# The scheduler orders the instructions of a two-layer diffusion trunk by its detailed timeline model in place of its simple one

## The chip, the cores and the metric

The kernel runs on one core of one Trainium2 chip. The metric is device time in microseconds. One execution was taken by the hardware profiler; the others were only timed.

## The reference

Two layers of a trunk are computed for two token groups that share one set of parameters: 128 context tokens and 512 latent tokens (a grid of 64 columns and 8 rows), 1024 features each. Cut to what matters, one layer is:

```
mod = silu(c) @ ada_w + ada_b                 # six vectors of 1024: shift, scale, gate, twice
h   = rms_norm(x) * (1 + scale) + shift
z   = h @ w_in                                # 2560 columns
ya  = bidirectional RG-LRU(conv(z), gate)     # sigmoid gates, exp, sqrt, two scans
yb  = neighbourhood attention (4 heads of 64) # the context tokens: plain attention
yc  = differential attention (4 heads, two components of 32)
x  += gate * (concat(ya, yb, yc) @ w_out)
u   = conv3(h2 @ ffn_up)                      # 5632 columns
x  += gate * ((gelu(u_gate) * u_val) @ ffn_down)
```

The outputs are the tokens of both groups, the final LRU states and the keys and values of the context tokens.

## The kernel before

Tokens lie along the free dimension: the residual stream `xt` holds the 1024 features as 8 tiles of 128 partitions by 640 tokens. Products are made with fp32r operands that are split into a high and a low part. For a weight, `unit` (L372) does this: ScalarE copies the raw weight into `wh`, VectorE subtracts it to get `wl`, each 128x1024, and each product then takes three matmuls (L272 to L274, L281 to L283, L1286 to L1288).

The mixer (`mixer`, L597) runs the LRU for four column groups (`lru_conv`, `lru_gates`, `lru_decay`, `lru_scan`, L666 to L725), the projections by 256 columns (`tok_chunk`, L817), the two attentions (`na_prompt` L959, `na_sample` L974, `df_run` L1135) and the output product. Its weights come as a list of 14 jobs, `jobs`, each a load and one or two units; `prep` starts the next one while the one before is in use. The FFN (`ffn`, L1227) first treats three column tiles directly and then, in a loop of 19 iterations per layer, computes one tile of 2x128 columns of `ffn_up` in seven partial products (`Up`, L1270, p1 to p7), a convolution and gelu (`conv`, L1330), and a part of `ffn_down` for the tiles made earlier (`d_quad`, L1373). The next tile's weights are prepared by `up_weights` (L569), the last of them in `Up.rest` (L1276). The product that makes the modulation (`ada_group`, L210) is spread over the mixer and the FFN as matmuls with four narrow weights side by side.

All loads go through SyncE's queue. Raw weights of all kinds (`raw_tile`, L93) share one tag with two buffers, intermediate tiles of 640 tokens share a tag with eight, and PSUM is split into 3 + 2 + 2 + 1 banks (m, s, t, and one for ada and o).

The order of the instructions isn't the program's text. The framework records the instructions, and when its context closes, it plays them through a model of the chip: whenever an engine is free there, it gets the ready instruction that has the smallest priority number, and a tile gets its buffer at that moment. The order in which each engine got its instructions becomes the program of that engine. The priority number counts up along the text. The kernel moves it with `later`:

```
def later(n):
    tc.cur_priority += n
    yield
    tc.cur_priority -= n
```

The offsets reach from -2000 for the products of a head after the first (`run`, L200) over -40 for `Up.rest` and +40 for `conv` to +700 for the second pair of `lru_scan`. `tc.issue_after(x)` keeps what a block issues on the engine of x behind x, and `act` (L657) chains the LRU's activations in one order. All of these are constraints or weights in the scheduler's choice; where they leave a choice open, the model's times decide which instruction is ready when an engine comes free.

## Time and profile before

| what | value |
|---|---|
| median of 3 runs | 1601.61 us (1600.32 to 1602.11) |
| the profiled execution's own time | 1599.11 us |
| its span, first to last instruction | 1597.3 us |
| instructions | 28596 |
| mean granted clock of TensorE | 0.995 |

The profiled execution is 2.5 us shorter than the median of the runs, and 1.8 us of its time lie outside the span. The engines are TensorE (PE, its weight loads PEld), VectorE (DVE), ScalarE (ACT), GpSimd (POOL) and SyncE (SP; SPq is its queue). A busy time adds up the stretches in which at least one instruction of the engine runs. Matmuls are pipelined, so one is shown longer than the distance to the next.

### The profile page before, as it was taken

How to read it: one execution, taken by the hardware profiler on the slowest of the kernel's cores; microseconds unless marked ns; L12 is line 12 of the kernel's file. 1: busy time of each engine (PE TensorE's matmuls, PEld its weight loads, DVE VectorE, ACT ScalarE, POOL GpSimd, SP SyncE). 2: the span in 40 equal slices, each digit the busy share in tenths (PEclk: the TensorE clock that was granted, in tenths of full speed). 3: DMA queues.
4: the chain of work that ended last, by engine and by line, in shares of the span. 5: the costliest groups of instructions: out<-in, count | busy, mean ns of one | idle time of the engine just before them, and what ended most of it. 6: DMA issues, size and time to landing. Idle time of an engine off the chain costs nothing.

```text
span 1597.3 us, 28596 instructions
## 1 busy us (share of the span) xinstructions
PE 1552.9 (97%) x11183; PEld 1453.3 (91%) x11183; DVE 1321.2 (83%) x2894; ACT 917.2 (57%) x1689; POOL 89.9 (6%) x78
## 2 busy tenths in 40 slices
PE   7999999899999999999999899999999999999998
PEld 6877788799999999999998777988999999999998
DVE  5886778978999888888897776788799998888884
ACT  5865558746655454445458666685466554444451
POOL 0310200100000000000012201010000000000000
PEclk8999999999999999999999999999999999999999
DMA  9556632121444333222244564220312322222221
GB/s 329 182 196 219 174 108 87 47 80 37 142 153 137 99 89 89 80 77 73 90 145 132 185 215 126 70 106 29 89 54 73 116 80 80 80 80 80 73 73 67
DMA packets 208069, 177.30 MB, mean 111 GB/s; under 512 B 47574, under 2 KB 197310, under 8 KB 201790
## 3 DMA queue, kind: packets, MB, share of 16 engines
q1 hardware_dynamic: 207934, 175.48, 35.6%
q8 instruction: 88, 1.44, 0.4%
q14 instruction: 47, 0.39, 0.1%
HBM read 165.12 MB, written 10.34 MB: 110 GB/s over the span
## 4 chain that ended last, share of the span: by engine, by line
PE 78%; DVE 9%; ACT 5%; DMA 4%; issue 3%; POOL 1%; SPq 1%; DVEq 0%; ACTq 0%; POOLq 0%
PE m L283 6%; PE m L281 6%; PE m L282 6%; PE m L1286 6%; PE m L1287 6%; PE m L1288 5%; PE s L283 4%; PE s L282 4%; PE s L281 4%; PE m L272 3%; PE m L274 3%; PE m L273 3%; PE t L1288 3%; PE t L1286 3%; PE t L1287 3%
## 5 line engine op out<-in xcount | busy, mean ns | idle before, releaser
L117 DVE TENSOR_TENSOR wl<-up,wh 128x1024 fp32r<-128x1024 f32 x126 | 153.6, 1223 | 40.5 <-ACT wh L110 39.6
L110 ACT ACTIVATE wh<-up 128x1024 fp32r<-128x1024 f32 x126 | 132.2, 1052 | 81.6 <-PE t L1288 40.3
L1344 DVE SCALAR_TENSOR_TENSOR u<-raw,vec,u 128x127 f32<-128x127 f32 x352 | 175.4, 544 | 0.8 <-ACT u L1338 0.8
L272 PE MATMUL m<-wh,h 128*128 128x256 f32 x480 | 140.0, 292 | 0.0
L274 PE MATMUL m<-wh,h 128*128 128x256 f32 x480 | 138.2, 288 | 0.0
L273 PE MATMUL m<-wl,h 128*128 128x256 f32 x480 | 137.2, 286 | 0.0
L281 PE MATMUL m<-act,wh 128*128 128x320 f32 (+2 forms) x376 | 116.8, 311 | 0.0
L282 PE MATMUL m<-act,wl 128*128 128x320 f32 (+2 forms) x376 | 116.5, 310 | 0.0
L283 PE MATMUL m<-act,wh 128*128 128x320 f32 (+2 forms) x376 | 116.4, 310 | 0.0
L281 PE MATMUL s<-act,wh 128*128 128x320 f32 (+2 forms) x376 | 116.3, 309 | 0.0
L283 PE MATMUL s<-act,wh 128*128 128x320 f32 (+2 forms) x376 | 116.2, 309 | 0.0
L282 PE MATMUL s<-act,wl 128*128 128x320 f32 (+2 forms) x376 | 115.9, 309 | 0.0
L283 PE MATMUL m<-h,wh 128*128 128x320 f32 (+2 forms) x352 | 111.7, 319 | 2.9 <-DVE h L117 1.7
L281 PE MATMUL m<-h,wh 128*128 128x320 f32 (+2 forms) x352 | 111.3, 317 | 1.0 <-DVE xt L541 0.7
L282 PE MATMUL m<-h,wl 128*128 128x320 f32 (+2 forms) x352 | 110.9, 315 | 0.0
L541 DVE SCALAR_TENSOR_TENSOR xt<-m,mod,xt 128x128 f32<-128x128 f32 (+3 forms) x224 | 90.5, 432 | 16.7 <-PE m L283 15.8
L272 PEld LDWEIGHTS m<-wh,h 128*128 128x128 f32 x480 | 91.7, 191 | 12.9 <-issue 11.6
L274 PEld LDWEIGHTS m<-wh,h 128*128 128x128 f32 x480 | 91.6, 191 | 3.2 <-issue 2.7
L1286 PE MATMUL m<-h,wh 128*128 128x320 f32 x304 | 94.4, 311 | 0.0
L273 PEld LDWEIGHTS m<-wl,h 128*128 128x128 f32 x480 | 91.7, 191 | 2.9 <-issue 2.9
L1288 PE MATMUL t<-tx,wh 128*128 128x320 f32 x304 | 94.1, 310 | 0.0
L1286 PE MATMUL t<-tx,wh 128*128 128x320 f32 x304 | 94.1, 310 | 0.0
(371 smaller groups left out, 4948.9 us busy)
## 6 DMA issues: line engine op xcount, KB each, us to landing
up<-in_ffn_up_dram SPq DMA_DIRECT2D x88, 512.0 KB
adaw<-in_ada_w_dram SPq DMA_DIRECT2D x40, 1024.0 KB
w<-in_w_in_dram SPq DMA_DIRECT2D x16, 1024.0 KB
rawd<-in_ffn_down_dram SPq DMA_DIRECT2D x24, 512.0 KB
pro<-in_ada_w_dram SPq DMA_DIRECT2D x30, 256.0 KB
w<-in_w_out_dram SPq DMA_DIRECT2D x8, 768.0 KB
rawd<-in_ffn_down_dram SPq DMA_DIRECT2D x16, 384.0 KB
xd<-xt SPq DMA_DIRECT2D x4, 1280.0 KB
```

The source lines that it names most:

```text
L110: return nc.scalar.activation(out, in_, AF.Copy)
L117: (eng or nc.vector).tensor_tensor(out, a, b, op=OP.subtract)
L272: nc.tensor.matmul(out, st[0], mv[0], start=(i == 0), stop=False)
L273: nc.tensor.matmul(out, st[0], mv[1], start=False, stop=False)
L274: nc.tensor.matmul(out, st[1], mv[0], start=False, stop=(i == n - 1))
L281: nc.tensor.matmul(out, a[0], b[0], start=(k == total[0]), stop=False)
L282: nc.tensor.matmul(out, a[1], b[0], start=False, stop=False)
L283: last = nc.tensor.matmul(out, a[0], b[1], start=False, stop=(k == total[-1]))
L1286: nc.tensor.matmul(ps, st[0], mv[0], start=first and k == 0, stop=False, skip_group_check=chk)
L1287: nc.tensor.matmul(ps, st[1], mv[0], start=False, stop=False, skip_group_check=chk)
L1288: nc.tensor.matmul(ps, st[0], mv[1], start=False, stop=last and k == 3, skip_group_check=chk)
L1344: nc.vector.scalar_tensor_tensor(u[:, oa:ob], r[:, oa + sft:ob + sft], w, u[:, oa:ob], op0=OP.mult, op1=OP.add)
```

## The change

The context in which the framework schedules gets one argument. With it, the framework plays the instructions through its detailed timeline simulator, which models an instruction as a list of events on separate parts (sequencer, engine, queues, semaphores, transfers) with contention for them, and not through its simple model. Instructions, tiles, buffer counts, priorities and edges are the same.

```
-    with tile.TileContext(nc) as tc:
+    with tile.TileContext(nc, schedule_with_timeline_sim=True) as tc:
         trunk_kernel(tc, ins, outs)
```

## Rows read from the trace of the kernel before

**Rows 1.** The page's first part: busy us (share of the span) xinstructions.

```profile
span 1597.3 us, 28596 instructions
...
PE 1552.9 (97%) x11183; PEld 1453.3 (91%) x11183; DVE 1321.2 (83%) x2894; ACT 917.2 (57%) x1689; POOL 89.9 (6%) x78
```

**Rows 2.** Busy time by stage; columns: stretch, length, busy us per engine, clock, DMA share.

```profile
0.00:40.00 40.00, 28.72 (x339) 24.29 (x343) 22.48 (x67) 21.69 (x44) 1.22 (x5) 0.87 1.01 329
40.00:310.00 270.00, 257.51 (x1985) 219.34 (x1978) 216.25 (x574) 187.00 (x401) 43.48 (x34) 0.99 0.46 146
310.00:520.00 210.00, 208.04 (x1423) 195.27 (x1424) 185.02 (x416) 118.58 (x207) 0.00 (x0) 1.00 0.36 111
520.00:800.00 280.00, 280.00 (x1926) 278.58 (x1925) 237.51 (x418) 135.44 (x203) 1.48 (x2) 1.00 0.28 84
...
840.00:1095.00 255.00, 241.81 (x1862) 206.05 (x1860) 197.84 (x520) 179.35 (x383) 39.05 (x33) 0.99 0.42 131
1095.00:1200.00 105.00, 103.90 (x723) 99.49 (x722) 88.74 (x226) 61.38 (x123) 0.00 (x0) 1.00 0.23 65
1200.00:1560.00 360.00, 360.00 (x2452) 359.50 (x2452) 319.38 (x549) 184.18 (x274) 0.00 (x0) 1.00 0.28 82
```

**Rows 3.** TensorE's waits: for whom, us in total, times, longest us.

```profile
PE s L273 <- DVE xs L117: 5.8, 4, 2.7
PE t L343 <- DMA cin<-in_c_ctx_dram: 3.3, 1, 3.3
```

**Rows 4.** Timeline near 110 and 902: start, us, what [idle before <-releaser].

```profile
110.53 0.28 PE L274 MATMUL m<-wh,h 128*128 128x256 f32 x1
...
110.65 0.34 PE L272 MATMUL s<-xs,gh 128*128 128x384 f32 x1
...
110.85 1.95 DVE L117 TENSOR_TENSOR xs<-xc,xs 128x640 fp32r<-128x640 f32 x1
...
112.85 0.39 PE L273 MATMUL s<-xs,gh 128*128 128x256 f32 x1 [1.62 <-DVE xs L117]
...
901.29 0.18 DVE L126 TENSOR_TENSOR rw<-rw,v 128x20 f32<-128x20 f32 x1
...
901.51 1.45 DVE L127 SCALAR_TENSOR_TENSOR r<-rw,r 128x20 f32<-128x20 f32 x1
...
905.04 0.82 DVE L117 TENSOR_TENSOR xs<-xc,xs 128x640 fp32r<-128x640 f32 x1
...
905.91 0.39 PE L273 MATMUL s<-xs,gh 128*128 128x256 f32 x1 [2.74 <-DVE xs L117]
```

**Rows 5.** Groups from 520 to 800: busy us, mean ns, idle before.

```profile
L1344 DVE SCALAR_TENSOR_TENSOR u<-raw,vec,u 128x127 f32<-128x127 f32 x114 | 57.3, 544 | 0.4 <-ACT u L1338 0.4
L117 DVE TENSOR_TENSOR wl<-up,wh 128x1024 fp32r<-128x1024 f32 x39 | 47.7, 1224 | 17.4 <-ACT wh L110 17.1
L110 ACT ACTIVATE wh<-up 128x1024 fp32r<-128x1024 f32 x39 | 40.9, 1049 | 15.8 <-PE t L1288 13.7 <-PE s L283 2.1
...
L117 DVE TENSOR_TENSOR act<-u,act 128x640 fp32r<-128x640 f32 x15 | 12.3, 819 | 1.6 <-ACT act L110 1.6
L1349 DVE TENSOR_TENSOR u<-u 128x640 f32<-128x640 f32 x15 | 12.3, 817 | 0.1
...
L117 DVE TENSOR_TENSOR up<-pT,up 128x512 f32<-128x512 f32 x13 | 8.9, 683 | 0.0
```

**Rows 6.** Waits from 520 to 800: us in total, times, longest us.

```profile
ACT raw L110 <- PE m L1288: 22.7, 24, 1.4
```

**Rows 7.** SyncE's queue over the span: its longest wait, and issues with sizes.

```profile
SPq L565 <- DVE u L1344: 368.0, 23, 17.0
...
adaw<-in_ada_w_dram SPq DMA_DIRECT2D x40, 1024.0 KB
```

**Rows 8.** ScalarE's groups: table loads of the LRU's line.

```profile
L658 ACT ACT_TABLE_LOAD x12 | 15.4, 1283 | 0.2
```

**Rows 9.** VectorE's groups over the whole span.

```profile
L117 DVE TENSOR_TENSOR ws<-pT,ws 128x512 fp32r<-128x512 f32 x38 | 26.2, 689 | 0.7
```

## The prediction

> **What bounds the kernel now.** I read the page's busy times first. TensorE's matmuls cover 1552.9 of the 1597.3 us span, so only 44.4 us are open in which another order of the same instructions could gain by closing gaps; VectorE is next with 83% [rows 1]. Then the busy time by stage [rows 2], which decides the case, because the room is very unevenly spread. TensorE's idle time is 11.3 us in the first 40 us, 12.5 in the first mixer (40 to 310), 2.0 in the ramp into the first FFN (310 to 520), 0.0 from 520 to 800, 13.2 in the second mixer (840 to 1095), 1.1 in the second ramp and 0.0 from 1200 to 1560. What is left of the 44.4, 4.3 us, lies at the seam of the layers and in the tail. The two flat stretches together are 640 us, 40% of the span, and there one 320-column matmul follows another every 280/1926 = 0.145 us. In them nothing can be gained by an order, only lost.

> Third, TensorE's own waits [rows 3]. The two largest of this list's 28 rows stand there. The reader is to see how short they are: no single wait in the list is over 3.3 us, and no row of it names a weight tile (wh, wl) as what was waited for. The longest inside the mixers is for xs, the low half of the LRU input. Fourth, the timeline around two of those waits [rows 4]: the xs subtraction takes 1.95 us at 110.85 although the same line takes 0.82 at 905.04, and in the second mixer it stands behind a small reciprocal-root step that took 1.45 us where its neighbours take 0.18. TensorE stood 1.62 and 2.74 us. Fifth, groups and waits of the flat stretch [rows 5, 6]: ScalarE and VectorE wait for TensorE (the evacuations of m, the buffers that t frees) and for one another, TensorE for neither.

> **What the change does.** No instruction, tile, byte or buffer count changes; only the order on each engine's queue, and with it which tile of a shared tag gets which buffer and when SyncE can issue a load. The order still follows the priorities (program order plus the offsets of `later`, the `issue_after` edges, the chain of `act`). What differs is the moment at which the scheduler believes an instruction to be ready and an engine to be free. So I cost by what comes late, not by what is added.

> Start, 0 to 40: the transfers' share is 1.01 of the 16 engines [rows 2]. It is bound by the bytes that the first matmuls need. Every buffer is free then, so the loads come in priority order by either model. Cost 0; bounds, 2 us each way.

> Mixers: each takes 14 weight jobs (the list `jobs`), 28 in both. A weight unit is one ScalarE copy and one VectorE subtraction, 1.05 + 1.22 = 2.27 us [rows 5]. Today none of the 28 is waited for [rows 3], since matmuls of other work cover it. A unit that is dealt behind one other unit comes 2.27 us late, and where TensorE's queue holds its matmuls next, TensorE stands that long, in order, with the transposes and score matmuls that VectorE and ScalarE wait for behind it. Lower bound: no job late and the present idle time halved, -(12.5 + 13.2)/2 = -12.9 us. Upper bound: the idle time doubles, +25.7. I take one job in five late, 28/5 = 5.6, call it 6: 6 x 2.27 = +13.6 us. That is between the ends and nearer to the loss, because weights are a hand-off that costs nothing now and can only become worse, while the waits that there are now stand partly on VectorE times (1.95 for 0.82, 1.45 for 0.18) that come from what else runs at that moment [rows 4] and that an order does not remove for sure.

> Ramps (310 to 520, 1095 to 1200): VectorE has 185.0 of 210 and 88.7 of 105 us [rows 2], little spare. One subtraction dealt late in each: 2 x 1.22 = +2.4 us. Bounds: -3.1 (all the idle time gone) and +6.

> FFN, flat part: 0. The cover is VectorE's idle time, 280 - 237.5 = 42.5 us in the first stretch. It holds 13 subtractions up<-pT, one to an iteration, so 42.5/13 = 3.3 us of spare each [rows 5]. A single late subtraction (1.22 us) stays under that. What it costs if the cover is gone is the first rival.

> SyncE: one queue issues every load in order, and it stands up to 17.0 us before an ffn_up load until VectorE is through with L1344 [rows 7]; the tag of these loads has two buffers. A different interleaving of ada_w with the FFN and mixer weights moves such a wait from one load to the next. An adaw load is 1024 KB [rows 7]. I put nothing extra here: in the mixers it would show as a late weight job, already counted.

> ScalarE's table loads: 1.28 us each; 12 of them belong to the LRU's activations [rows 8]. If exponentials and sigmoids are dealt more finely, three more per mixer are 6 x 1.28 = 7.7 us of ScalarE, which has 187.0 of 270 and 179.4 of 255 us in the mixers. So I take 0, upper bound +7.7.

> Sum: 0 + 13.6 + 2.4 + 0 = +16.0 us on the profiled execution's 1599.1, so 1615.1. The median of the runs shown is 1601.6, 2.5 above the profiled one; carried over it is about 1617.

> **The rivals.** *FFN cover lost (slower, much).* For each column tile the convolution issues eight multiply-adds, 57.3 x 8/114 = 4.0 us in the first flat stretch, and two passes of 0.82 us, together 5.6 us of VectorE [rows 5]. If the new order puts this block ahead of the next unit's weight preparation, it exceeds the 3.3 us of spare by 2.3 us in an iteration. There are 38 iterations [rows 9]; with the full block in half of them it is 19 x 2.3 = 44 us: about 1646. It decides as soon as what is put ahead is more than 3.3 us. Against it: the offsets -40 and +40 of `rest` and `conv` hold in either order.

> *Hand-offs filled (faster).* If the detailed model sees the delay between a producer and its consumer, it deals other matmuls into the present gaps of the mixers. Halving them gives -12.9, and half of the ramps' 3.1 about -1.5: 1587. For it: the pieces that TensorE could run there exist (the gate matmuls and the projection alternate one by one in [rows 4]). It decides as long as fewer than six weight jobs come late for it, since six cost 13.6.

> *More room than the matmul row shows (faster still).* In the mixers TensorE's weight loads cover only 219.3 of 270 and 206.1 of 255 us, against 278.6 of 280 in the flat stretch [rows 2]. So 99.6 us of the mixers pass with no weight load under way, of which the matmul row shows 25.7 as idle. A fifth of this won by denser dealing is -20: 1582. [...]

> *Nothing measurable.* The priorities leave so little choice that the two orders are nearly equal, or losses and gains cancel: 1598.4 to 1604.8, which is 0.2% either way, about what a measurement of this kernel can tell from no change. Against it: with 28596 instructions and several streams ready at once, the orders in the mixers can't stay equal.

> **How the numbers follow.** Forecast (some weight jobs late in the mixers, 1606 to 1632) 0.41, FFN cover lost 0.15, hand-offs filled 0.23, more room 0.08, nothing measurable 0.13. Slower: 0.41 + 0.15 = 0.56; same 0.13; faster 0.23 + 0.08 = 0.31. The predicted time is that of the likeliest, 1617. Its own range is 1606 to 1632. The range for 8 in 10 has to take in cases of both signs: below, most of the hand-off case and half of the room case, 1582; above, half of the cover case, 1645.

> **What would show it.** Right: TensorE's idle time in the two mixers grows from 25.7 to about 40 us; rows appear among its waits that name wl, wh or a DMA into w; the flat stretches keep 0.145 us per matmul. The cover case: TensorE is no longer at 280 of 280 in the FFN, with waits for wl behind VectorE's u. The faster cases: the mixers' idle time falls and so does the time at which the first flat stretch begins (about 520) and the distance between the two FFNs. The prediction would be wrong if the detailed model happens to place VectorE's small steps better than the simple one, because then the xs waits of [rows 3] go without any weight coming late.

## The result, and the profile after

The changed kernel takes 1759.5 us (median of 4 runs, 1755.2 to 1763.0) against 1601.0 us before (median of 4, the profiled execution among them): a ratio of 1.0988 (95% interval 1.0964 to 1.1012), 159 us slower. That is outside the predicted range of 1582 to 1645 us. The forecast was 1617 us. It had the direction, and the mixers as the place; the size was ten times too small.

The first part of the page after answers to [rows 1]:

```profile
span 1761.2 us, 28587 instructions
...
PE 1619.5 (92%) x11183; PEld 1511.1 (86%) x11183; DVE 1319.1 (75%) x2894; ACT 925.8 (53%) x1691; POOL 86.4 (5%) x78
```

TensorE has the same 11183 matmuls. Its idle time is 1761.2 - 1619.5 = 141.7 us, 97.3 more than the 44.4 of before, and its busy time is 66.6 us longer. VectorE, ScalarE and GpSimd are within 9 us of what they had. So the span's 163.9 us are two terms: TensorE standing still, and TensorE taking longer for the same work.

The busy time by stage puts both in the same places. It answers to [rows 2], with the stretches cut at the same events (the first and last instruction of each FFN's L1286); columns as there.

```profile
0.00:40.00 40.00, 29.23 (x360) 22.17 (x360) 22.14 (x66) 21.49 (x44) 1.27 (x5) 0.91 0.99 327
40.00:380.00 340.00, 299.00 (x2089) 259.28 (x2087) 221.34 (x585) 194.58 (x403) 40.49 (x34) 0.89 0.40 125
380.00:494.00 114.00, 94.67 (x592) 88.51 (x592) 84.16 (x222) 57.91 (x121) 0.00 (x0) 0.85 0.11 32
494.00:869.00 375.00, 373.20 (x2543) 364.03 (x2543) 319.70 (x575) 186.87 (x276) 0.00 (x0) 1.00 0.35 104
...
920.00:1250.00 330.00, 290.91 (x2054) 253.19 (x2052) 218.06 (x553) 194.14 (x400) 40.11 (x35) 0.90 0.35 111
1250.00:1361.00 111.00, 92.63 (x569) 86.67 (x568) 82.79 (x216) 56.71 (x119) 0.00 (x0) 0.85 0.12 33
1361.00:1724.00 363.00, 362.00 (x2466) 361.74 (x2465) 316.05 (x544) 183.88 (x272) 0.00 (x0) 1.00 0.28 81
```

TensorE's idle time in the two mixers (40 to 380 and 920 to 1250) is 41.0 + 39.1 = 80.1 us, where before had 12.5 + 13.2 = 25.7. In the two ramps behind them it is 19.3 + 18.4 = 37.7 us. The same ramps of before, cut at the first L1286 (310 to 414 and 1095 to 1198), have 1.25 + 1.1 = 2.35. These four stretches hold 89.8 of the 97.3 us. They are also where the granted clock fell: 0.85 to 0.90, with 0.99 to 1.00 before. The two FFNs take 375 and 363 us at a clock of 1.00, where before needed 370 (414 to 784) and 357 us (1198 to 1555). The first FFN begins at 494 instead of 414 (+80), and from its last L1286 matmul to the first of the second FFN it is 492 instead of 414 us (+78).

TensorE's waits over the whole span answer to [rows 3]; columns: for whom, us in total, times, longest us.

```profile
PE t L203 <- ACT pT L110: 21.6, 15, 2.3
PE s L1079 <- DVE e L1081: 10.0, 19, 1.4
PE m L281 <- ACT h L110: 7.8, 2, 3.9
PE s L273 <- DVE xs L117: 7.4, 2, 4.3
...
PE m L281 <- ACT wh L110: 4.4, 2, 2.2
...
PE t L343 <- DMA cin<-in_c_ctx_dram: 3.2, 1, 3.2
```

The xs wait of [rows 3] grew from 5.8 to 7.4 us. The two rows on top were small before: the scores had waited for e for 1.7 us in 7 waits, and that kernel's list has no row of L203 for pT. Both are attention chains: the values (L203) wait for the evacuated transposes pT, the scores (L1079) for VectorE's pass from the accumulator s into e (L1081), which frees the accumulator for the next scores. Late weights, the theory of the prediction, are among the rows, but small: all rows that name wh come to 8.9 us in 5 waits, and none names wl.

**Where the cover went.** The first layer again, cut by the steps of the chains: the LRU with its gates (up to the last activation of L658, a square root), the first attention (up to the first score of L1079), the second attention (up to the last one), the ramp. First all engines of after in the first three, then in all four the matmuls into the accumulator tag m alone (columns: stretch, length, TensorE busy with its count, clock, DMA share, GB/s). Ahead of the FFN these are the projections and the output product. I call them filler, the matmuls that can stand between the steps of the chains; not all are free to move, since the LRU's own input (132 in the first stretch of either kernel) and the output product hang on the chains.

```profile
40.00:165.00 125.00, 117.26 (x863) 106.86 (x859) 82.74 (x172) 80.24 (x129) 19.24 (x13) 0.95 0.55 173
165.00:270.00 105.00, 85.87 (x616) 68.70 (x612) 61.53 (x166) 47.61 (x126) 14.29 (x17) 0.84 0.43 128
270.00:391.00 121.00, 104.64 (x658) 90.36 (x658) 84.80 (x280) 73.62 (x166) 6.96 (x4) 0.86 0.19 62
```

```profile
40.00:165.00 125.00, 94.81 (x668) 0.95 0.55 173
165.00:270.00 105.00, 40.35 (x256) 0.84 0.43 128
270.00:391.00 121.00, 55.12 (x336) 0.86 0.19 62
391.00:494.00 103.00, 52.08 (x266) 0.87 0.12 35
```

The same steps in the kernel before: the matmuls into m, and all engines for the first three stretches.

```profile
40.00:132.00 92.00, 67.02 (x468) 1.00 0.61 199
132.00:233.00 101.00, 60.56 (x412) 1.00 0.53 160
233.00:320.00 87.00, 52.45 (x270) 0.98 0.20 69
320.00:414.00 94.00, 65.05 (x376) 1.00 0.21 61
```

```profile
40.00:132.00 92.00, 88.63 (x667) 77.90 (x662) 82.30 (x166) 70.08 (x114) 22.87 (x13) 1.00 0.61 199
132.00:233.00 101.00, 96.36 (x794) 78.65 (x793) 67.52 (x171) 54.59 (x139) 12.70 (x17) 1.00 0.53 160
233.00:320.00 87.00, 82.48 (x612) 72.11 (x612) 75.33 (x268) 68.90 (x164) 7.90 (x4) 0.98 0.20 69
```

Both kernels have 1526 matmuls into m from 40 us to the first FFN (668 + 256 + 336 + 266 and 468 + 412 + 270 + 376). After deals 668 of them into the LRU, before 468. The 200 more are projections for the attentions (m<-wh,h at L272 to L274: 536 in this stretch, 336 before). VectorE is busy for the same 82 us in the stretch of either kernel, but it takes 125 us for it instead of 92: TensorE, busy for 117 of the 125, is doing projections that are wanted later, and the gates queue behind them. The last gate matmul ends at 152.5 us, before at 119.3. Between the gates and VectorE stands ScalarE with the sigmoids, and it waited longer for the gates, 19.8 us in 18 waits here and 5.0 in 9 before (first after, 40 to 165; then before, 40 to 132):

```profile
ACT i L658 <- PE s L274: 13.4, 9, 3.5
ACT r L658 <- PE s L274: 6.4, 9, 2.1
```

```profile
ACT r L658 <- PE s L274: 3.7, 5, 1.5
ACT i L658 <- PE s L274: 1.3, 4, 0.7
```

Then the stock is short: 256 instead of 412 are left for the first attention, where TensorE is busy for 85.87 of 105 us at a clock of 0.84, and 266 instead of 376 for the ramp.

A short stock is half of the story. By length the four stretches lost 33, 4, 34 and 9 us, and the second attention, which lost most, has more matmuls into m than before, 336 against 270. There it is again their place that costs: between its first and its last score they stand in blocks of 12 in the median, 4 before, the scores queue behind the blocks, and VectorE waits for the scores (row `DVE e L1081 <- PE s L1079`) for 12.3 us in 12 waits (270 to 391) instead of 4.9 in 9 (233 to 320). TensorE is idle for 16.4 us of this stretch, before for 4.5.

The timeline of TensorE in the first attention of after shows the steps bare: values, scores, transposes (start, us, what, in brackets the idle time before and what ended it).

```profile
213.80 0.88 PE L203 MATMUL t<-pT,naset 128*64 128x128 f32 x12 [1.51 <-ACT pT L110]
214.60 0.92 PE L203 MATMUL s<-naset 64*128 64x256 f32 x8
215.46 0.88 PE L950 MATMUL t<-ident,p 128*128 128x128 f32 x6
218.27 0.88 PE L203 MATMUL t<-pT,naset 128*64 128x128 f32 x12 [1.93 <-ACT pT L110]
```

The same steps in the kernel before, where the lines left out between the transposes and the next values are projections:

```profile
182.04 0.88 PE L203 MATMUL t<-pT,naset 128*64 128x128 f32 x12
...
183.70 0.87 PE L950 MATMUL t<-ident,p 128*128 128x128 f32 x6
...
186.45 0.88 PE L203 MATMUL t<-pT,naset 128*64 128x128 f32 x12
```

One round of the chain takes 4.47 us after (213.80 to 218.27, both values) and 4.41 us before (182.04 to 186.45). Later rounds of after are longer, up to 6.29 us (4.60 before); the last six of the seven come to 29.0 us after and 26.2 before. So the chain is hardly slower here. What differs is what TensorE has to do in the 2 us until ScalarE, which has exponentials to do as well, has evacuated pT: projections before, nothing after. They had been spent earlier, where they delayed the gates.

ScalarE's table loads of L658 (14 of them, 12 in [rows 8]) and SyncE's queue complete the picture: neither shows as a bound of TensorE.

```profile
L658 ACT ACT_TABLE_LOAD x14 | 18.0, 1283 | 8.1 <-DVE r L121 5.6 <-DVE th L722 2.3
```

```profile
SPq L565 <- DVE u L1344: 309.6, 21, 15.4
SPq L565 <- DVE wl L117: 236.7, 14, 51.3
```

The longest wait of SyncE is 51.3 us now. Before it was 30.0 us, in a row of L536: the 17.0 of [rows 7] is the longest of the row that is largest in total, and not, as its heading says, of the queue. But the list of TensorE's waits names transfers with 3.7 us at most in one row.

### The profile page after: what moved, and what is told of

Read it like the earlier page. It is cut to its first block, busy times and chain, and to the rows that moved or that the text cites. A ratio compares the mean times of both kernels' runs of the same rounds, so it can differ in the third digit from the quotient of the medians.

```text
span 1761.2 us, 28587 instructions
## 1 busy us (share of the span) xinstructions
PE 1619.5 (92%) x11183; PEld 1511.1 (86%) x11183; DVE 1319.1 (75%) x2894; ACT 925.8 (53%) x1691; POOL 86.4 (5%) x78
## 4 chain that ended last, share of the span: by engine, by line
PE 76%; DVE 11%; ACT 5%; DMA 4%; issue 2%; POOL 1%; SPq 1%; DVEq 0%; ACTq 0%; POOLq 0%
PE m L283 7%; PE m L282 6%; PE m L281 6%; PE m L1287 5%; PE m L1288 5%; PE m L1286 5%; PE s L283 4%; PE s L281 4%; PE s L282 4%; PE m L272 3%; PE m L273 3%; PE m L274 3%; PE t L1286 2%; PE t L1288 2%; PE t L1287 2%
## 5 line engine op out<-in xcount | busy, mean ns | idle before, releaser
L1344 DVE SCALAR_TENSOR_TENSOR u<-raw,vec,u 128x127 f32<-128x127 f32 x352 | 176.3, 543 | 0.2 <-ACT u L1338 0.2
L110 ACT ACTIVATE raw<-m 128x320 f32<-128x320 f32 x126 | 55.0, 437 | 198.1 <-PE m L1288 176.5
L272 PE MATMUL m<-wh,h 128*128 128x256 f32 x480 | 139.5, 292 | 2.3 <-DVE v L836 2.3
L274 PE MATMUL m<-wh,h 128*128 128x256 f32 x480 | 139.2, 290 | 0.0
L272 PEld LDWEIGHTS m<-wh,h 128*128 128x128 f32 x480 | 94.7, 198 | 7.4 <-issue 3.7
L274 PEld LDWEIGHTS m<-wh,h 128*128 128x128 f32 x480 | 94.7, 197 | 6.0 <-issue 6.0
L1286 PE MATMUL t<-tx,wh 128*128 128x320 f32 x304 | 94.2, 310 | 1.0 <-ACT wh L110 1.0
L1287 PE MATMUL m<-h,wl 128*128 128x320 f32 x304 | 94.1, 310 | 0.0
```

The costliest lines, as they stand in the source:

```text
L110: return nc.scalar.activation(out, in_, AF.Copy)
L272: nc.tensor.matmul(out, st[0], mv[0], start=(i == 0), stop=False)
L274: nc.tensor.matmul(out, st[1], mv[0], start=False, stop=(i == n - 1))
L1286: nc.tensor.matmul(ps, st[0], mv[0], start=first and k == 0, stop=False, skip_group_check=chk)
L1287: nc.tensor.matmul(ps, st[1], mv[0], start=False, stop=False, skip_group_check=chk)
L1344: nc.vector.scalar_tensor_tensor(u[:, oa:ob], r[:, oa + sft:ob + sft], w, u[:, oa:ob], op0=OP.mult, op1=OP.add)
```

## The experiments

Every experiment computes the whole of the kernel; only orders change. The windows are set like this, here for the first one:

```
+    depth = dict(TRN2Spec.ENG_ISSUE_QUEUE_DEPTH)
+    TRN2Spec.ENG_ISSUE_QUEUE_DEPTH = {**depth, E.PE: 2}
     with tile.TileContext(nc, schedule_with_timeline_sim=True) as tc:
         trunk_kernel(tc, ins, outs)
+    TRN2Spec.ENG_ISSUE_QUEUE_DEPTH = depth
```

All medians are of 4 runs beside 7 runs of the kernel before on the same chip (1601.5 to 1603.4 us).

**TensorE's window alone: 2, 16, 70.**

> The detailed model, with TensorE's issue window in the model (how many instructions its sequencer hands on before the engine has done them) set from 35 to 2 while the order is made; no other part of the model changes. Theory W (window): with 35, the scheduler must commit about 17 filler matmuls before it learns that the next step of a chain (gate, softmax, value) is ready, so each step of the chains of the mixers is dealt some 20 matmuls late, the filler is used up early, and the second half of the chains runs bare. W expects most of the loss back: 1590 to 1640 us, TensorE's idle time over the span down from 141.7 to under 75 us, and runs of 1 to 8 filler matmuls between gate steps instead of about 20. Theory O (the order on VectorE, ScalarE and SyncE and the buffers that go with it): 1720 to 1770. Theory C (the model's TensorE clock, which it halves at rest): 1720 to 1770.

> The same with a window of 16. W expects a loss between those of 2 and 35, about in proportion to the window: 1650 to 1710 us. O and C expect the time of the changed kernel, 1740 to 1770.

> The same with a window of 70. W expects more loss than with 35, chain steps some 40 matmuls apart: 1820 to 1950 us. O and C expect 1740 to 1770.

| TensorE's window | us | ratio to before (95%) | TensorE busy | idle | clock | run between gates | first to last gate |
|---|---|---|---|---|---|---|---|
| 2 | 1645.0 | 1.0267 (1.0242 to 1.0292) | 1562.7 | 82.9 | 0.973 | 6 | 67.8 |
| 16 | 1685.7 | 1.0523 (1.0503 to 1.0543) | 1585.8 | 99.6 | 0.960 | 9.5 | 73.1 |
| 35 (the change) | 1759.5 | 1.0988 (1.0964 to 1.1012) | 1619.5 | 141.7 | 0.937 | 18 | 83.5 |
| 70 | 1804.5 | 1.1270 (1.1244 to 1.1295) | 1632.7 | 169.5 | 0.934 | 36 | 97.6 |

Busy and idle are from the profiled execution (idle is span less busy). The last two columns are counted in TensorE's timeline of the first layer: how many other matmuls stand in a row between two groups of gate matmuls (those into s at L272 to L274), in the median, and the us from the first gate matmul to the end of the last. The kernel before has 3 and 60.7 us. Both columns grow with the window at every step. At 35 and 70 the run is half the window, about the 17 and not far from the 40 that were expected; at 2, 18 of the 28 runs are of 8 matmuls or fewer, where 1 to 8 had been expected of all. The second attention, from first to last score, grows as well: 96.6, 111.6, 121.0 and 127.2 us, 87.3 before. With nothing else touched the time follows the window through four sizes. The two outer sizes missed the expected ranges, by 5 us above and 16 below, and at 2 the idle time of 82.9 us missed the expected 75: 2 leaves 43 us unexplained, and 70 costs less than twice 35.

**The other engines' windows alone: 12 to 1, TensorE's at 35.**

> TensorE's window stays at 35 in the model; those of VectorE, ScalarE and GpSimd go from 12 to 1. W expects little: 1730 to 1775 us. O expects most of the loss back: 1600 to 1660. C expects 1740 to 1770.

1733.7 us, ratio 1.0828 (1.0805 to 1.0851). That is inside W's range and far from O's. These windows are worth 26 us where TensorE's is left open.

**TensorE's order alone.** The kernel is ordered by the detailed model, the resulting order of TensorE's instructions is kept by name, and the kernel is built once more with the simple model and TensorE held to that order; then the reverse. The links that hold the order add no semaphore.

```
+    for a, b in zip(names, names[1:]):
+        tc.add_manual_dep(by[b], a, DependencyInfo(NoSync, DATA), reason="order")
...
+    order = build(_bacc, data, True)[2]
+    nc, arrays, _ = build(_bacc, data, False, order)
```

> TensorE's instructions stand in the order that the detailed model gave them, name by name; the other engines' and the DMA queues' order is left to the simple model. Window theory (the loss is the order on TensorE, filler ahead of the next step of a chain): 1730 to 1790 us, with about 140 us of idle TensorE. Theory of the other engines (the loss is the order on ScalarE and VectorE or of the transfers): 1600 to 1650 us.

1782.3 us, ratio 1.1127 (1.1104 to 1.1150). TensorE's order by itself carries the whole loss, and 23 us more. Its idle time is 1780.9 - 1619.8 = 161.1 us, where about 140 had been expected. The page and the waits of this run:

```profile
PE 1619.8 (91%) x11183; PEld 1510.2 (85%) x11183; DVE 1311.8 (74%) x2894; ACT 925.6 (52%) x1690; POOL 81.2 (5%) x78
```

```profile
PE t L203 <- ACT pT L110: 25.1, 16, 2.8
...
PE s L1079 <- DVE e L1081: 9.2, 18, 1.3
```

Busy time is that of the changed kernel and the two attention waits are near it (21.6 and 10.0 us there), with the other engines in an order that the simple model made.

> The reverse: TensorE in the order of the kernel before, the rest ordered by the detailed model. Window theory: 1595 to 1640 us, with TensorE's idle time near 44 us and the granted clock near 0.99. Theory of the other engines: 1720 to 1770 us.

1677.6 us, ratio 1.0474 (1.0449 to 1.0499): a miss for both theories, with TensorE idle for 95.9 us at a clock of 0.974. Putting TensorE back in its old order gives back 82 of 159 us, not all.

So TensorE's new order is enough for the loss, and undoing it isn't enough for the gain: the detailed model's order of the other engines costs 76 us beside a TensorE order that it didn't choose.

**The clock in the model.** The model's TensorE is never at its slow clock; the windows stay at 35 and 12.

```
+    TRN2Spec.PE_CLOCK = dataclasses.replace(clock, resting=TRN2Spec.PE_CYCLE)
```

> The detailed model with its TensorE never at the slow clock in the model, its windows as they are (35 and 12). If the model misplaces the chain because it believes TensorE slow after a pause (clock theory): 1600 to 1680 us. Window theory: no change of more than 15 us from 1759, so 1745 to 1775 us.

1762.7 us, ratio 1.1001 (1.0971 to 1.1032). The clock theory falls.

**All windows closed: TensorE 2, the other three 1.**

> The detailed model with a window of 2 on TensorE and of 1 on ScalarE, VectorE and GpSimd. Window theory, if the 43 us that stayed with TensorE's window at 2 (1645 us) are the other engines' windows: 1600 to 1625 us. If they come from something else in the detailed model (its durations, and so which transfer or buffer it thinks comes first): 1635 to 1655 us.

1616.0 us, ratio 1.0086 (1.0062 to 1.0110): the expected 1600 to 1625. Of the 159 us the windows hold 144. The busy time by stage of this run, cut as above, without the FFNs (first mixer, ramp, second mixer, ramp):

```profile
40.00:315.00 275.00, 259.56 (x2034) 229.59 (x2033) 215.36 (x574) 190.33 (x398) 42.76 (x34) 1.00 0.47 149
315.00:418.00 103.00, 92.11 (x635) 87.99 (x634) 83.91 (x221) 60.37 (x124) 0.00 (x0) 0.95 0.17 50
...
830.00:1112.00 282.00, 268.04 (x2091) 237.48 (x2091) 220.77 (x586) 195.96 (x410) 40.98 (x35) 1.00 0.43 135
1112.00:1212.00 100.00, 89.02 (x600) 85.43 (x597) 79.75 (x206) 57.24 (x118) 0.00 (x0) 0.93 0.17 47
```

The mixers are nearly back (15.4 and 14.0 us idle). The first FFN begins at 418, where before has 414, and from its last L1286 matmul to the second FFN it is 421 us, where before has 414. Most of the idle time that is left over stands in the ramps: 10.9 + 11.0 us, where before has 2.35. And the stock is spread almost as in the kernel before; the matmuls into m over the same four steps of this run:

```profile
40.00:139.00 99.00, 69.00 (x479) 1.00 0.61 193
139.00:232.00 93.00, 56.68 (x402) 1.00 0.54 166
232.00:328.00 96.00, 69.55 (x379) 1.00 0.21 73
328.00:418.00 90.00, 50.27 (x264) 0.94 0.18 52
```

479 and 402 in the LRU and the first attention (468 and 412 before). Only behind them it differs: 379 for the second attention and 264 for the ramp, with 270 and 376 before, and the ramp is where this kernel's TensorE still stands.

**Whose other window.** TensorE 2, ScalarE and GpSimd 1, VectorE back at 12.

> TensorE's window at 2, ScalarE's and GpSimd's at 1, VectorE's at its 12. It lies between 1616 us (all closed) and 1645 us (all three open): if VectorE's window carries the 29 us, since the gate steps xs, h and gl that TensorE waits for are made there, 1636 to 1650 us; if it is ScalarE's, 1612 to 1624 us.

1632.3 us, ratio 1.0196 (1.0170 to 1.0222): between the two answers. VectorE's window accounts for 16 of the 29 us, so about half; the rest is ScalarE's and GpSimd's.

**In between.** TensorE 4, the other three 2.

> TensorE's window at 4, ScalarE's, VectorE's and GpSimd's at 2. If the time only grows with the windows (41 us from 2 to 16 on TensorE, 29 us from 1 to 12 on the others): 1616 plus 6 plus 3, so 1620 to 1632 us. If it has a lowest point above the smallest windows, since a window of 1 on every engine gave 2127 us: under 1613 us, and perhaps under the 1602 us of the kernel before.

1624.4 us, ratio 1.0126 (1.0103 to 1.0149), as expected from growth with the windows. No setting that was run beats the kernel before.

**TensorE's old order, the other windows closed.**

> As the run with TensorE in the order of the kernel before and the rest ordered by the detailed model (1678 us), but with the model's windows of ScalarE, VectorE and GpSimd at 1 instead of 12. If the 76 us that were lost there are these windows: 1600 to 1625 us. If they are the price of ordering the rest round a foreign TensorE order, whatever the window: 1660 to 1690 us.

1653.7 us, ratio 1.0327 (1.0306 to 1.0349): a miss for both. The windows explain 24 of those 76 us. For the other 52 I have no run; the waits of this one are short and scattered (6.0 us in the largest row).

**Every window at 1.** SyncE's and TensorE's too. SyncE's has no part in what follows: with it at 12 the scheduler gives every engine the same order.

> Every window of the detailed model at 1, SyncE's and TensorE's too. Window theory: 1600 to 1616 us, a little under the 1616 us with TensorE at 2. If the 14 us that are left come from the model's durations: 1611 to 1625 us, no gain.

2127.5 us, ratio 1.3299 (1.3261 to 1.3338): the largest miss. A window of 1 on TensorE costs in every stage: the first FFN begins at 583 us (418 with a window of 2), 570 us pass between the two FFNs (421), and it breaks the second FFN, which all other runs left whole. The first one takes 396 us (372). The second one, and TensorE's and VectorE's largest waits over the span:

```profile
1549.00:2074.00 525.00, 398.78 (x2431) 392.86 (x2431) 317.22 (x528) 182.15 (x270) 0.00 (x0) 0.86 0.19 56
```

```profile
PE s L1286 <- DVE xt L541: 122.7, 23, 7.2
```

```profile
DVE wl L117 <- ACT wh L110: 216.5, 90, 26.7
DVE pT L572 <- DMA up<-in_ffn_up_dram: 101.2, 38, 4.9
```

The second FFN takes 525 us where before takes 357 and the change 363, which is a third of what this run loses. The next up-weights come late, VectorE waits for them (216.5 us in 90 waits for wh, 101.2 in 38 for loads of up), and behind these waits in VectorE's order stands the addition into xt that frees TensorE's accumulator, for which TensorE waits up to 7.2 us. The runs between the gates are the shortest of all here, 1 in the median, so filler ahead of the gates doesn't explain this loss. Why the model orders so with a window of 1 wasn't tried; the window theory in its simple form (smaller is better) is wrong below 2.

## Why the prediction was wrong

**Start, FFN, SyncE, table loads at 0: right.** The start is 29.23 us busy of 40, 28.72 before. In the FFN's flat part one 320-column matmul follows another as before: 362.00/2466 = 0.147 us over the whole second FFN, 357.0/2433 = 0.147 before. The two FFNs take 5 and 6 us more, against a forecast of 0 and a rival of 44, and that is work moved into them: 34 and 33 more matmuls (2543 and 2466 against 2509 and 2433), 5 us each at 0.147. The waits of SyncE moved from one load to another, as said (L565 waits less for u, 309.6 instead of 368.0 us, and more for wl). The table loads grew by 2.6 us of an engine with room.

**Mixers +13.6: the step that failed.** It was costed as weight jobs that come late, 6 of 28, with "the idle time doubles" as its upper bound. Late weights did come, 5 waits and 8.9 us in all rows that name wh, so that mechanism is real and was sized near what it cost. It wasn't the one that mattered, and that the forecast had the right sign is in part luck: the loss came another way. The forecast's place between its bounds also leaned on VectorE times put down to what else runs at that moment. What made them long is not shown: of the eight xs subtractions in the trace before, two took 1.95 and 1.96 us and six 0.81 to 0.82. The two overlap a GpSimd step of L701, for 1.26 and 1.96 us, but one of the six does so too, for all its 0.81 us. After, all eight took 0.81 to 0.83 us. The mixers' idle time went from 25.7 to 80.1 us, three times instead of at most twice. The working had the fact in hand that would have shown it: none of the weights was waited for "since matmuls of other work cover it". I asked what an order might do to the weights and not what it might do to the cover. The matmuls into m ahead of the FFN are a fixed stock, 1526 in the first layer. An order that deals 200 of them too many among the gates delays the gates and leaves the first attention and the ramp bare; in the second attention the blocks in which they stand delay the scores. For the bound, the right row was not TensorE's idle time of now but the length of the chains: in [rows 2] VectorE, which carries them, has work for 216 of 270 us, and a round of the first attention takes 4.4 us with about 2 in which TensorE has nothing of its own. I worked out no bound from these rows, so whether one would have held the 159 us stays open.

**Ramps +2.4: the same error.** They were costed by one late subtraction each, and their idle time grew by 35.3 us. They begin with what the mixer left over, and the cover was gone there too. In the run with all windows closed they still have 19.6 us more idle time than before, where the whole span has 26.5 us more.

**No term for the clock.** 66.6 of the span's 163.9 us are longer busy time for the same matmuls. No step had such a term, although [rows 2] showed a stretch of it: 0 to 40, where TensorE is busy for 28.72 of 40 us, at a granted clock of 0.87 of full speed, beside 0.99 and more elsewhere. A mean clock of 0.937 over 1761 us is 2 x 0.063 x 1761 = 222 us at half speed if the rest is at full; by the same working before has 16 (0.995). The traces list two levels, 1 and 0.5 of full speed: after ran at 0.5 for 225.5 us, with TensorE busy in 177.1 of them; before did for 18.8, busy in 16.3. From 49.75 to 50.61 us of after, at 0.50, one 256-column matmul follows another every 0.215 us, and from 54.22 to 55.89, at 1.00, every 0.119. By these two, 1 - 0.119/0.215 = 0.45 of 177.1 - 16.3, 72 us, is an estimate of what the lower clock added, against 66.6 measured in all; by it the order itself took some busy time away, as in the run with all windows closed. In this run each microsecond of new idle time came with about 0.7 us of longer busy time (66.6/97.3). That is no constant: with TensorE's window at 2 it is 9.8/38.5 = 0.25, and with all windows closed the busy time fell.

**The rivals.** FFN cover lost: no, the cover held at 1.00 and 275 matmuls per 40 us. Hand-offs filled: no; the idle time of the mixers grew threefold. Nothing measurable: no. More room than the matmul row shows: the run with all windows closed does the 11183 matmuls in 1540.7 us of busy time, 12.2 less than before, with weight loads busy for 229.59 of 275 us in the first mixer where before has 219.34 of 270. So some such room is there, but the idle time grew by 26.5 and the kernel is slower: no order that was run turned the 12.2 us into a shorter time.

**What is shown and what is not.** Shown: the time follows TensorE's window through 2, 16, 35 and 70; TensorE's new order alone, under the simple model, costs at least as much as the change; with the windows nearly closed 144 of 159 us are gone; the clock in the model has no part. That the filler ahead of the gates and scores is the way in which a wide window costs is read from the runs between gates, which grow with the window through four sizes, and from the tables by stage of three kernels; it was not isolated further (no run moved the filler alone). Open: the last 14 us, the 52 us beside TensorE's old order, and the break at a window of 1.

## What to carry to other kernels

Where a chain of small steps and a stock of independent matmuls share TensorE, the order decides how the stock is spread, and no count of late hand-offs bounds that: a better upper bound may be the length of the chain without any cover, from the engine that carries it, which this case did not try. When a scheduler's model is swapped, look first at how far ahead it commits work, and compare the number of filler instructions between two steps of a chain; the busy time by stage shows it as a full engine beside a chain's own engine that takes longer for the same work (here TensorE busy for 117 of 125 us beside VectorE, which did in these 125 us the 82 that it had done in 92). And give new idle time on TensorE a term for the lower clock; here it was anywhere from nothing to 0.7 us for each microsecond.

## What the runs showed of the hardware

In five orders the same 11183 matmuls were busy for 1540.7 us at a mean granted clock of 0.990, 1552.9 at 0.995, 1585.8 at 0.960, 1619.5 at 0.937 and 1725.6 at 0.883. The clock was low in stages in which TensorE stood idle for a good part of the time: 0.84 in the first attention of after (idle for 19.1 of 105 us), a mean over parts at full and at half speed, 0.85 in its first ramp (19.3 of 114) and 0.95 in the first ramp of the run with all windows closed (10.9 of 103). In that run's first mixer, idle for 15.4 of 275 us, it was 1.00. In the second FFN of the run with every window at 1, with 126.2 of 525 us idle and a clock of 0.86, a matmul took 398.78/2431 = 0.164 us of busy time, where the second FFN of before takes 357.0/2433 = 0.147.
